# Attention with exponentials on two engines: eleven groups on VectorE instead of ten, and one pass of the last on GpSimd

## The chip, the core and the metric

The kernel runs on one core of a Trainium2 chip. A core has five engines that run side by side, each with its own queue of instructions, in order: TensorE (PE; its weight loads are listed as PEld), VectorE (DVE), ScalarE (ACT), GpSimd (POOL) and SyncE (SP, which issues most DMAs here). They wait for each other through semaphores. The metric is device time in microseconds (us); lower is better. The profile is one execution, recorded by the hardware profiler.

## The reference

Attention over 8 x 8 heads, 512 positions, 64 dimensions, all float32:

```
scale = 1.0 / np.sqrt(q.shape[-1])
scores = np.einsum('bhqd,bhkd->bhqk', q, k) * scale
scores = scores - scores.max(axis=-1, keepdims=True)
attn = np.exp(scores)
attn = attn / attn.sum(axis=-1, keepdims=True)
return np.einsum('bhqk,bhkd->bhqd', attn, v)
```

So there are 64 x 512 x 512 = 16.8 million exponentials. The kernel leaves out the subtraction of the maximum, which cancels in the division.

## The kernel before, in words

**Tiling.** Heads come in 32 pairs. Of a pair, q, k and v are loaded as 128x512 float32 tiles (256 KB each) by SP, and cast to float16 by GpSimd (`cast`, lines 435 and 445). q and k are transposed on TensorE (line 469, eight 128x128 matmuls for a pair) into a PSUM bank and copied to SBUF by VectorE (`copy`, line 482, tile `tqk`). A score block is 128 keys by 512 queries of one head; four blocks make a head. Two blocks make a *group*, 128x1024 scores in a PSUM tile `st` (three buffers). There are 129 groups, numbered from 0; the last two are halves of one (256 queries each), so that the end is short. Groups 0 to 2 are written out by hand (`first_pair`).

**Exponentials.** For most groups ACT computes exp(scale x score) in one instruction from `st` to a float16 tile `pt` (line 516). For the groups in `ON_DVE` (line 34, ten of them) VectorE does it by arithmetic on bits: TensorE first writes a constant into `st` (line 497, the lift) and adds the scores to it; then `raise_` (line 533) scales and clamps `st` into a float32 tile `z`, which frees `st`; then three passes (`pass_`, line 550) form a polynomial of z's low 16 bits: the first (f + c0) x f into `y`, the second (y + c1) x y into `y`, the third c2 x y + z as an integer into `pd`, of which one half of each word is the float16 result. `z` and `y` have two buffers each, `pd` has four.

**Values.** For each head and each quarter of the queries, four matmuls (`values`, line 585) multiply `pt` or `pd` with v, to which a column of ones is appended, so that the sum of the exponentials comes with the output. Seven such units of 65 columns share a PSUM bank; VectorE takes the reciprocal of the sums (line 563) and multiplies (line 565) into a ring in SBUF, and SP stores each finished head from there. The two PSUM banks `x0` and `x1` serve transposes and outputs in turn. The last head has code of its own (`last_values`, line 601, and `finish`, lines 615 and 616).

**What sets the order.** All instructions are emitted in an order that a planner in the kernel's own Python (`Plan`) fixes beforehand: it goes through time in steps of 5 ns with constants for how long each thing takes, and notes when which step would be issued. Its times are not waits: on the chip each engine runs its own instructions in that order, held by data dependences only. PE's steps are chosen in `step_pe` (scores when a buffer is free and ACT's backlog is small, else transposes of a pair up to `AHEAD` ahead, else values). VectorE's are chosen in `step_dve`: first copies that are due, then raises, then the others in order of readiness; passes fill the rest, as long as no other job would be more than `LATE_NORM` or `LATE_COPY` late. GpSimd's casts are placed behind a pass of VectorE, when possible (`emit`, `cast_behind`), and each cast brings with it the load of the pair seven further on, on SP's queue, in which the stores stand too. `EXP` and `EXP_FIXED` are what one exponential on ACT takes in the plan, `SLOT` one group's scores on PE, `PASS` a pass, `port` the time up to which a pass or a cast has SBUF's port in the plan.

Of the kernel before, what the change touches and what calls it, by code (L numbers as in the profile page):

```python
# [16 lines left out]

class Plan:

    SLOT, EXP, EXP_DONE, EXP_FIXED = 216, 853, 181, 50  # L20
    INTO, OUT_OF = 95, 105
    TRANSPOSE, V_UNIT = 225, 130
    TO_ACT, TO_DVE, TO_PE = 220, 210, 60

    COPY, NORM, RAISE = (601, 690), (307, 390), (1132, 1215)
    COPY_1 = (400, 190)
    NORM_COLUMN, PASS_DONE = 67, 80
    PASS, PASSES = 1133, 3
    OFFSET = 216
    FIRST_EXP = 4915  # L30
    STEP = 5
    CALM, KEEN = 14000, 6
    FIRST_UNIT = 4
    ON_DVE = (8, 21, 29, 40, 54, 65, 77, 85, 90, 106)

    LATE_NORM, LATE_COPY, HURRY, SOON, BACKLOG = 600, 1800, 900, 80, 1200
    SLACK, AHEAD = 0, 1

    CAST, CAST_DONE, TO_POOL = 557, 130, 150
    FIRST_LAND, LOAD, STORE, LATENCY, ISSUE = 5200, 700, 350, 2300, 450  # L40
    RAW, QK16, NV = 7, 5, 12

# [68 lines left out]
    def step_pool(self, t):  # L111
        if self.uncast and self.uncast[0][1:] != (1, "q") and not self.casts and self.pool <= t:
            quiet = not self.passes and self.port <= t and not any(x[1] == "raise" for x in self.ready)
            if self.fits(t) and (quiet or self.uncast[0][0] - 1500 < t):
                self.emit(t, None)
        if self.casts and self.pool <= t and self.port <= t:
            g, n, after = self.casts[0]
            if after <= t and self.landed.get((g, n), 1e9) <= t:
                self.casts.pop(0)
                self.pool = t + self.CAST  # L120
                self.port = t + self.CAST
                self.cast_done[(g, n)] = t + self.CAST + self.CAST_DONE
# [153 lines left out]
    def step_dve(self, t):  # L276
        if self.uncast and self.uncast[0][1:] == (1, "q"):
            if self.landed.get((1, "q"), 1e9) <= t:
                self.emit(t, None)
                self.dve = t + 240  # L280
                self.pool = self.port = t + 330
                self.cast_done[(1, "q")] = t + 400
            return
        now = [x for x in self.ready if x[0] <= t]
        if now:
            g = self.groups[min(self.m + 1, len(self.groups) - 1)][0][0]
            job = min(now, key=lambda x: (x[1] != "copy" or x[2][0] > g, x[1] != "raise", x[0]))
            self.ready.remove(job)
            _, kind, what = job
            slots = 2 if kind == "raise" else 1  # L290
            while slots and not self.casts and self.fits(t, 60 if slots == 1 else 0):
                self.emit(t, self.dve_done if self.dve_done > t - 300 else None)
                slots -= 1
                if slots and self.fits(t, 500):
                    self.emit(t, self.dve_done if self.dve_done > t - 300 else None)
                    slots -= 1
            self.note(t, kind, *what)
            if kind == "norm":
                more = self.NORM_COLUMN * what[1]
                self.dve = t + self.NORM[0] + more  # L300
                self.banks[what[2]] = t + self.NORM[1] + more + self.TO_PE
                for _ in range((what[0] + what[1]) // 4 - what[0] // 4):
                    self.loads.append(("store", self.dve + 100))
            elif kind == "finish":
                self.dve = t + self.NORM[0] + 2 * self.NORM_COLUMN
            elif kind == "copy":
                held, done = self.COPY if what[0] != 1 else self.COPY_1
                self.dve = t + held
                self.banks[what[1]] = self.tq[what[0]] = t + done + self.TO_PE
            else:  # L310
                self.dve = t + self.RAISE[0]
                self.read[what[0]] = t + self.RAISE[1] + self.TO_PE
                self.passes += [(what[0], s) for s in range(self.PASSES)]
            self.dve_done = self.dve
        elif self.passes:
            m, s = self.passes[0]
            end = max(t, self.port) + self.PASS
            late = {"copy": self.LATE_COPY, "norm": self.LATE_NORM, "raise": self.LATE_NORM, "finish": 0}
            if all(x[0] > end - late[x[1]] for x in self.ready):
                self.passes.pop(0)  # L320
# [22 lines left out]
def kernel(  # L343
# [7 lines left out]
    nc = tc.nc  # L351
# [191 lines left out]
    def pass_(m, s):  # L543
# [181 lines left out]
    with tc.manual_schedule():  # L725
# [9 lines left out]
        for n in range(NV):  # L735
# [8 lines left out]
            "raise": raise_,  # L744
            "copy": lambda g, b: copy(g),
            "pass": pass_,
            "last": last_values,
            "finish": finish,
            "norm": lambda u, n, b: normalise(u, n),
# [33 lines left out]
```

## Time and profile before

| | us |
|---|---|
| median of three runs | 118.86 (118.70 to 118.92) |
| the profiled execution | 118.68 |
| its span, first to last instruction | 116.9 |
| mean granted clock of TensorE | 1.000 |

Busy times of all engines, the costliest lines and the stages are shown with the prediction. How to read them: a line of the kernel is L and its number; "out<-in" are tiles by the program's names with buffer numbers left out, then partitions x elements and type. "x10" is a count. In a timeline the columns are start and duration in us, then what ran; instructions of one kind that follow each other stand in one row with their count. In a list of waits stand the engine and line, what ended the wait, then us in total, times and the longest. In a table of stages each engine has its busy time and, in brackets, its instructions that start in the stage. In a line's own view stand the shortest, median and longest duration in ns, and below who waited for it (us, times). Records of ACT overlap: an instruction's record begins when its operands are there, while the one ahead still runs.

### The profile page before, as it was taken

The page shows a single profiled execution, that of the slowest core. Times are in us where ns is not written, and L with a number is a line of the kernel's source. Part 1 is how long each engine was busy: PE and PEld are TensorE (multiplying, and loading weights), DVE is VectorE, ACT ScalarE, POOL GpSimd, SP SyncE. Part 2 cuts the span into 40 slices and gives each one's busy share as a digit, 9 for nine tenths or more (in the row PEclk, how much of TensorE's full clock was granted, in tenths as well). Part 3 has the DMA queues.
Part 4 walks back from the last instruction along what each step waited for, and adds up shares of the span by engine and source line. Part 5 has one row for each costly group of instructions (what it writes and reads, how often), then busy time and mean ns, then how long its engine had stood idle before and what let it go on. Part 6 is the DMA issues. An engine that isn't in the chain of part 4 may idle for free.

```text
span 116.9 us, 4082 instructions
## 1 busy us (share of the span) xinstructions
PE 105.0 (90%) x1579; PEld 66.4 (57%) x1579; DVE 98.1 (84%) x174; ACT 110.6 (95%) x123; POOL 57.9 (50%) x102
## 2 busy tenths in 40 slices
PE   7969996987998999898997999999989998999980
PEld 2626553664655666455754575565556665667460
DVE  3453997699899999999999969899978999996281
ACT  4599999999999999999999999999999999999980
POOL 2369925844725844355592595549246454442000
PEclk9999999999999999999999999999999999999999
DMA  3999999999999999999899998899999996232254
GB/s 100 288 374 380 379 383 383 385 376 374 359 338 332 346 346 336 320 303 358 229 327 302 301 299 276 244 325 268 329 356 313 320 309 225 78 117 98 89 176 134
DMA packets 35604, 33.83 MB, mean 289 GB/s; under 512 B 2688, under 2 KB 35584, under 8 KB 35584
## 3 DMA queue, kind: packets, MB, share of 16 engines
q1 hardware_dynamic: 35152, 33.24, 86.9%
q10 hardware_dynamic: 432, 0.33, 0.9%
q8 instruction: 12, 0.20, 0.7%
q14 instruction: 8, 0.07, 0.2%
HBM read 25.17 MB, written 8.39 MB: 287 GB/s over the span
## 4 chain that ended last, share of the span: by engine, by line
ACT 52%; PE 25%; DVE 11%; issue 9%; ACTq 0%
ACT pt L516 50%; PE st L511 9%; PE o L585 9%; DVE y L550 3%; PE st_0a L634 3%; PE tp L469 2%; ACT pt L684 2%; DVE z L533 2%; DVE tqk L482 2%; DVE ring L565 2%; DVE pd L550 1%; PE st L497 1%; DVE rc L563 1%; DVE obl L616 0%; DVE rc_last L615 0%
## 5 line engine op out<-in xcount | busy, mean ns | idle before, releaser
L516 ACT ACTIVATE pt<-st 128x1024 f16<-128x1024 f32 (+1 forms) x116 | 105.7, 1279 | 0.0
L511 PE MATMUL st<-tqk 64*128 64x512 f16 (+1 forms) x250 | 45.6, 380 | 5.2 <-ACT pt L516 3.7
L585 PE MATMUL o<-vp,pt 128*128 128x65 f16 x928 | 42.3, 194 | 0.4 <-DVE tqk L482 0.2
L585 PEld LDWEIGHTS <-pt 128*128 128x128 f16 x928 | 35.6, 98 | 12.0 <-issue 10.9
L445 POOL CAST qkp<-k 128x512 f16<-128x512 f32 x31 | 19.0, 614 | 16.6 <-DVE rc L563 3.9
L435 POOL CAST vp<-v 128x512 f16<-128x512 f32 x32 | 19.6, 616 | 15.4 <-DVE y L550 7.6
L445 POOL CAST qkp<-q 128x512 f16<-128x512 f32 x30 | 18.4, 614 | 13.2 <-DVE pd L550 5.4
L565 DVE TENSOR_TENSOR ring<-o,rc 128x448 f32<-128x448 f32 (+2 forms) x37 | 22.6, 612 | 1.5 <-DVE rc L563 0.3
L511 PEld LDWEIGHTS <-tqk 64*128 64x128 f16 x250 | 13.1, 93 | 18.2 <-issue 10.5
L482 DVE COPY tqk<-tp 128x1024 f16<-128x1024 f16 x30 | 20.5, 683 | 1.0 <-PE tp L469 1.0
L469 PE MATMUL tp<-ident,qkp 128*128 128x128 f16 x248 | 19.9, 220 | 1.2 <-DVE tqk L482 0.6
L469 PEld LDWEIGHTS <-qkp 128*128 128x128 f16 x248 | 14.1, 97 | 9.8 <-issue 4.9
L533 DVE TENSOR_SCALAR z<-st 128x1024 f32<-128x1024 f32 x10 | 12.2, 1221 | 2.5 <-PE st L511 2.2
L563 DVE RECIPROCAL rc<-o 128x7 f32<-128x7 f32 (+2 forms) x37 | 7.4, 199 | 6.8 <-PE o L585 6.4
L550 DVE SCALAR_TENSOR_TENSOR y<-y 128x1024 f32<-128x1024 f32 x10 | 12.4, 1240 | 0.0
L550 DVE SCALAR_TENSOR_TENSOR y<-z 128x1024 f32<-128x1024 uint16 x10 | 12.3, 1232 | 0.1
L550 DVE SCALAR_TENSOR_TENSOR pd<-y,z 128x1024 uint32<-128x1024 f32 x10 | 12.2, 1218 | 0.0
L585 PE MATMUL o<-vp,pd 128*128 128x65 f16 x80 | 11.8, 195 | 0.0
L585 PEld LDWEIGHTS <-pd 128*128 128x128 f16 x80 | 7.8, 98 | 1.5 <-issue 0.8
L497 PE MATMUL st<-const-bfloat16-1.0,lift 64*128 64x512 bf16 x20 | 3.9, 380 | 0.8 <-ACT pt L516 0.6
L634 PE MATMUL st_0a<-const-bfloat16-1.0 128*128 128x512 bf16 (+1 forms) x11 | 3.5, 482 | 0.8 <-PEq L767 0.8
L634 PEld LDWEIGHTS <-const-bfloat16-1.0 128*128 128x128 bf16 x15 | 1.7, 129 | 2.4 <-issue 2.4
(48 smaller groups left out, 22.1 us busy)
## 6 DMA issues: line engine op xcount, KB each, us to landing
out_dram<-ring SPq DMA_DIRECT2D x63, 128.0 KB, 3.9
k<-in_k_dram SPq DMA_DIRECT2D x31, 256.0 KB, 5.3
q<-in_q_dram SPq DMA_DIRECT2D x31, 256.0 KB, 5.1
v<-in_v_dram SPq DMA_DIRECT2D x27, 256.0 KB, 5.4
v<-in_v_dram SPq DMA_DIRECT2D x10, 128.0 KB, 4.0
k<-in_k_dram ACTq DMA_DIRECT2D x2, 128.0 KB, 2.8
q<-in_q_dram SPq DMA_DIRECT2D x2, 128.0 KB, 2.6
out_dram<-obl SPq DMA_DIRECT2D x1, 64.0 KB, 1.6
```

Of the source, the lines that this page charges most:

```text
L435: return nc.gpsimd.tensor_copy(out=vps[g % NV][:, :, :, 0:D], in_=raw[g]["v"][:, :, :, :])
L445: return nc.gpsimd.tensor_copy(out=dst, in_=src[:, :, :, :])
L469: nc.tensor.transpose(tps[g][:, n, i, :], qkp[g][:, n, i, :], ident)
L482: nc.vector.tensor_copy(out=tqk[g][:, :, :], in_=tps.pop(g).rearrange("p n i c -> p n (i c)"))
L511: nc.tensor.matmul(st[:, x, cols], kc, qc[:, cols], start=not on_dve, stop=True)
L516: nc.scalar.activation(out=pt[:, :, cols], in_=st[:, :, cols], func=EXP, scale=scale)
L533: nc.vector.tensor_scalar(out=r["z"][:, :, :], in0=r["st"][:, :, :], scalar1=STEP, scalar2=2.0**17, op0=AluOp.mult, op1=AluOp.max,)
L550: nc.vector.scalar_tensor_tensor(out=r["bits"][:, :, :] if last else r["y"][:, :, :], in0=r["y"][:, :, :] if s else f, scalar=QUARTIC[s], ...
L563: nc.vector.reciprocal(out=rc[:, 0:n], in_=o[:, x : x + n, D : D + 1])
L565: nc.vector.tensor_tensor(out=ring[:, u % NU : u % NU + n, :], in0=o[:, x : x + n, 0:D], in1=rc[:, 0:n].broadcast_to([P, n, D]), op=AluOp. ...
L585: nc.tensor.matmul(os[u // 7][:, u % 7, :], blocks[(g, c, h)][:, y * P : (y + 1) * P], vps[g % NV][:, h, c, :], start=(c == 0), stop=(c == ...
L634: nc.tensor.matmul(dst[:, 0:n], ones[:, 0:P], ones[:, 0:n], start=True, stop=True)
```

## The change

Places and constants in `Plan`; a new job that is planned among GpSimd's casts; and its code. Group 112, the last of the eleven in the new list (`SHARED` = 1), has its middle pass on GpSimd: an addition (`tensor_scalar`, y + c1, times 1.0) into a new tile `t`, and a product of `t` and `y` back into `y`. In the plan that job takes 1000 + 2250 ns, holds the port, and the third pass becomes ready 250 ns behind it. `AHEAD` goes from 1 to 2.

```diff
-    SLOT, EXP, EXP_DONE, EXP_FIXED = 216, 853, 181, 50
-    INTO, OUT_OF = 95, 105
-    TRANSPOSE, V_UNIT = 225, 130
-    TO_ACT, TO_DVE, TO_PE = 220, 210, 60
+    SLOT, EXP, EXP_DONE, EXP_FIXED = 226, 865, 165, 52
+    INTO, OUT_OF = 96, 97
+    TRANSPOSE, V_UNIT = 226, 128
+    TO_ACT, TO_DVE, TO_PE = 206, 215, 60
...
-    PASS, PASSES = 1133, 3
+    PASS, PASSES = 1131, 3
-    FIRST_EXP = 4915
+    FIRST_EXP = 5130
-    ON_DVE = (8, 21, 29, 40, 54, 65, 77, 85, 90, 106)
+    ON_DVE = (7, 20, 28, 40, 51, 56, 70, 80, 84, 98, 112)
+    SHARED = 1
-    LATE_NORM, LATE_COPY, HURRY, SOON, BACKLOG = 600, 1800, 900, 80, 1200
-    SLACK, AHEAD = 0, 1
-    CAST, CAST_DONE, TO_POOL = 557, 130, 150
+    LATE_NORM, LATE_COPY, HURRY, SOON, BACKLOG = 1000, 2200, 900, 80, 1200
+    SLACK, AHEAD = 0, 2
+    CAST, CAST_DONE, TO_POOL = 560, 130, 150
+    MIDDLE, MIDDLE_DONE = (1000, 2250), 250
...
             g, n, after = self.casts[0]
-            if after <= t and self.landed.get((g, n), 1e9) <= t:
+            if g == "middle" and after <= t:
+                self.casts.pop(0)
+                self.pool = self.port = t + sum(self.MIDDLE)
+                self.passes[self.passes.index((n, 2, 1e9))] = (n, 2, self.pool + self.MIDDLE_DONE)
+            elif after <= t and self.landed.get((g, n), 1e9) <= t:
...
-        elif self.passes:
-            m, s = self.passes[0]
+        elif any(x[2] <= t for x in self.passes):
+            m, s, _ = job = next(x for x in self.passes if x[2] <= t)
...
+                if s == 0 and m in self.ON_DVE[len(self.ON_DVE) - self.SHARED :]:
+                    self.passes.remove((m, 1, 0))
+                    self.passes[self.passes.index((m, 2, 0))] = (m, 2, 1e9)
+                    self.casts.append(("middle", m, end + self.TO_POOL))
+                    self.note(end, "middle", m)
...
+    def middle(m):
+        y = raised[m]["y"]
+        t = wpool.tile([P, 2, S], FP32, tag="t", name=f"t_{m}", bufs=1)
+        nc.gpsimd.tensor_scalar(
+            out=t[:, :, :], in0=y[:, :, :], scalar1=QUARTIC[1], scalar2=1.0, op0=AluOp.add, op1=AluOp.mult
+        )
+        nc.gpsimd.tensor_tensor(out=y[:, :, :], in0=t[:, :, :], in1=y[:, :, :], op=AluOp.mult)
```

More of the change, by code (lines that the diff above doesn't have):

```diff
@@ L312, in step_dve @@
                 self.read[what[0]] = t + self.RAISE[1] + self.TO_PE
-                self.passes += [(what[0], s) for s in range(self.PASSES)]
+                self.passes += [(what[0], s, 0) for s in range(self.PASSES)]
             self.dve_done = self.dve
-        elif self.passes:
-            m, s = self.passes[0]
+        elif any(x[2] <= t for x in self.passes):
+            m, s, _ = job = next(x for x in self.passes if x[2] <= t)
             end = max(t, self.port) + self.PASS
@@ L319, in step_dve @@
             if all(x[0] > end - late[x[1]] for x in self.ready):
-                self.passes.pop(0)
+                self.passes.remove(job)
                 self.note(t, "pass", m, s)
                 self.dve = self.port = self.dve_done = end
+                if s == 0 and m in self.ON_DVE[len(self.ON_DVE) - self.SHARED :]:
[3 more added lines that the diff above has]
+                    self.note(end, "middle", m)
                 if s == self.PASSES - 1:
@@ L746 @@
             "pass": pass_,
+            "middle": middle,
             "last": last_values,
```

## The prediction

> **What bounds the kernel now.** I read the page's first part, then the waits and the timeline of ScalarE (ACT), then the instructions of one source line, and last a table of stages. Nothing else than ACT can be the bound if its chain has no holes, so that comes first.
>
> ```profile
> PE 105.0 (90%) x1579; PEld 66.4 (57%) x1579; DVE 98.1 (84%) x174; ACT 110.6 (95%) x123; POOL 57.9 (50%) x102
> ```
>
> ```profile
> ACT L650 <- PEq L767: 1.7, 1, 1.7
> ...
> ACT pt L684 <- PE st_0a L677: 0.4, 1, 0.4
> ```
>
> ```profile
> 6.05 1.95 ACT L684 ACTIVATE pt<-st 128x1024 f16<-128x1024 f32 x2
> 7.86 105.73 ACT L516 ACTIVATE pt<-st 128x1024 f16<-128x1024 f32 x116
> ```
>
> ```profile
> L516 ACT ACTIVATE pt<-st x116: 1017/1293/1501, 7.9 to 112.5; 128x1024 f16<-128x1024 f32 x114, 128x512 f16<-128x512 f32 x2
> ...
>   PE st L511: 3.7, 10
>   PE st L497: 0.6, 2
> ```
>
> ACT's list of waits ends before its first exponentials; for line 516 it has none. The 116 instructions of that line are one stretch of records without a hole, from the end of the two before (6.05+1.95 = 8.00) to 7.86+105.73 = 113.59. Two of them are halves; counted as one, 105.59/115 = 0.918 us is the price of one exponential of 128x1024. A record is longer than that (median 1.293) because it begins while its predecessor still runs: the input was there in time. The reverse wait exists: PE waits for ACT to free a score buffer, 3.7+0.6 us. So the time is: start (8.0), 115 x 0.918, and about 3.3 us of last values, division, store and closing (113.59 to the span's 116.9). The chain view's many pieces of PE and DVE in the middle follow early starts of records; none of them delayed an end.
>
> How near the others are to being the bound, by stage:
>
> ```profile
> core 0: us, PE busy (x) PEld busy (x) DVE busy (x) ACT busy (x) POOL busy (x), PEclk, DMA share, GB/s
> 8.00:24.00 16.00, 14.21 (x208) 8.89 (x208) 11.79 (x19) 15.99 (x18) 11.22 (x20) 1.00 1.09 381
> 24.00:44.00 20.00, 18.27 (x280) 11.86 (x278) 19.15 (x30) 20.00 (x23) 10.78 (x18) 1.00 1.05 353
> 44.00:64.00 20.00, 18.16 (x288) 11.40 (x288) 19.57 (x29) 20.00 (x23) 9.97 (x17) 1.00 0.99 309
> 64.00:84.00 20.00, 18.91 (x290) 11.99 (x290) 18.47 (x30) 20.00 (x24) 12.57 (x22) 1.00 0.94 291
> 84.00:104.00 20.00, 19.09 (x310) 12.53 (x310) 18.61 (x30) 20.00 (x24) 9.57 (x16) 1.00 0.78 255
> 104.00:113.00 9.00, 8.84 (x158) 5.94 (x154) 5.56 (x12) 9.00 (x12) 0.77 (x2) 1.00 0.33 108
> ```
>
> DVE is the neighbour: 75.80 of 80 us from 24 to 104, so 4.20 idle, and 3.44 idle from 104 to 113. What ended its idle time in the long stretch was mostly PE:
>
> ```profile
> DVE rc L563 <- PE o L585: 1.5, 5, 0.6
> DVE tqk L482 <- PE tp L469: 1.0, 1, 1.0
> DVE z L533 <- PE st L511: 0.3, 1, 0.3
> ```
>
> **The change, part by part.** (1) *One exponential of 128x1024 leaves ACT*: -0.92 us, on the path.
>
> (2) *PE* gets one more pair of lift products (line 497) ahead of the group's scores:
>
> ```profile
> 11.30 0.39 PE L497 MATMUL st<-const-bfloat16-1.0,lift 64*128 64x512 bf16 x2
> 11.52 0.70 PE L511 MATMUL st<-tqk 64*128 64x512 f16 x4
> ```
>
> 0.22 us, once. PE's 4.3 us of waiting for ACT hide it, and the 0.92 us by which ACT gets shorter; 3.2 us of that waiting would be left. Without cover it costs its 0.22. Taken as 0.
>
> (3) *DVE* gets a raise (line 533) and two passes (line 550); the third goes to POOL. From the end of the last group's work before:
>
> ```profile
> 86.86 1.22 DVE L550 SCALAR_TENSOR_TENSOR pd<-y,z 128x1024 uint32<-128x1024 f32 x1
> 87.99 0.68 DVE L482 COPY tqk<-tp 128x1024 f16<-128x1024 f16 x1
> ...
> 93.28 1.21 DVE L533 TENSOR_SCALAR z<-st 128x1024 f32<-128x1024 f32 x1
> 94.41 0.68 DVE L482 COPY tqk<-tp 128x1024 f16<-128x1024 f16 x1
> 95.01 1.24 DVE L550 SCALAR_TENSOR_TENSOR y<-y 128x1024 f32<-128x1024 f32 x1
> ...
> 96.94 1.22 DVE L550 SCALAR_TENSOR_TENSOR pd<-y,z 128x1024 uint32<-128x1024 f32 x1
> ...
> 98.68 1.23 DVE L550 SCALAR_TENSOR_TENSOR y<-z 128x1024 f32<-128x1024 uint16 x1
> ...
> 101.66 1.22 DVE L550 SCALAR_TENSOR_TENSOR y<-y 128x1024 f32<-128x1024 f32 x1
> ...
> 104.16 1.21 DVE L550 SCALAR_TENSOR_TENSOR pd<-y,z 128x1024 uint32<-128x1024 f32 x1
> ```
>
> From start to next start a pass or a raise takes 1.13 (86.86 to 87.99, 93.28 to 94.41), so 3 x 1.13 = 3.39 us are added. Old groups 8 and 21 and new groups 7 and 20 lie before 24 us, so the whole added group falls into the long stretch, but for its last pass, which comes behind 104 (below): 2.26 us against an idle 4.20, of which the shorter stretch takes 0.92. Left: 1.02 us of 79, if DVE can use all idle time. Of the idle, 2.8 us was waiting for PE; a backlog of passes fills such holes, and places close together (51 and 56, 80 and 84) make a backlog. Bounds: 0 when every hole is filled, 1.8 us lost when none of the 2.8 can be used (2.8 - 1.02). I take 0.1, near the lower end, because the old kernel already ran 20 us at 19.57 busy without a hole in ACT, with two dense places of its own (77, 85, 90).
>
> (4) *The middle pass on POOL*, addition and product. POOL in this trace has only casts and fills:
>
> ```profile
> 0.24 0.10 POOL L767 MEMSET const-float32-0.0<- 128x1 f32 x1 [0.24 <-issue]
> ...
> 1.01 0.29 POOL masks.py:199 TENSOR_SCALAR_AFFINE_SELECT ident<-ident 128x128 f16<-128x128 f16 x1
> 3.42 0.38 POOL L651 CAST k<-k 128x128 f16<-128x128 f32 x1 [2.12 <-DMA k<-in_k_dram]
> 4.00 0.61 POOL L653 CAST q<-q 128x512 f16<-128x512 f32 x1 [0.20 <-DMA q<-in_q_dram]
> ```
>
> Slope (0.61-0.38)/384 = 0.60 ns an element, so 1024 elements take at least 0.61+512 x 0.60 = 0.92; two such, 1.84, are the lower bound. The upper one lets each of the three streams that are read cost two whole casts: 3 x 1.22 = 3.66. I take 3.2, near the upper, since the product reads two. Where does it lie? New group 112 comes six groups after old group 106; one more of the groups ahead of it is on DVE, so five exponentials, 4.6 us, later: its raise starts near 93.28+4.6 = 97.9. The old group needed 104.16+1.21-93.28 = 12.1 us from raise to last pass, because the passes of the group before it and copies and divisions lay between. Between its first pass's end (98.68+1.23 = 99.91) and its last pass's start (104.16) were 4.25 us, of which the middle pass took 1.13 and other work the rest. POOL's 3.2 fits in these 4.25 beside that work, so the last pass would end at 97.9+12.1-1.13 = 108.9 (109.5 with the upper bound plus hand-overs). Its pair's values follow:
>
> ```profile
> 107.83 0.84 PE L511 MATMUL st<-tqk 64*128 64x512 f16 x4
> ...
> 109.22 1.28 PE L511 MATMUL st<-tqk 64*128 64x512 f16 x4
> 110.43 1.20 PE L585 MATMUL o<-vp,pt 128*128 128x65 f16 x32
> ```
>
> 32 matmuls, 1.20 us, in a tail where ACT ends at 112.7. PE has room there: four of its score matmuls take 1.28 once and 0.84 once, where 0.70 does in the row at 11.52; that is 0.72 us idle. Cost 0, to 1.20 if nothing is hidden; I take 0.05, near 0, since 3.8 us lie between 108.9 and ACT's end.
>
> The Trainium skill (GPSIMD Engine Reference, Performance versus the Vector engine) gives a two-input fp32 addition of 2048 elements 4497 ns on GpSimd against 2293 on VectorE, because two reads share one port. No row here shows a two-input operation on POOL. By half of it the product would take 2.25 and, as an estimate, the sum of the tail would not change. Its section When to use GPSIMD advises against elementwise work of two inputs there for that reason; here VectorE, not GpSimd, is the scarce one by the table of stages.
>
> What is queued behind the middle on POOL are casts:
>
> ```profile
> 102.94 0.61 POOL L445 CAST qkp<-q 128x512 f16<-128x512 f32 x1 [1.48 <-DMA out_dram<-ring]
> 103.54 0.62 POOL L435 CAST vp<-v 128x512 f16<-128x512 f32 x1
> 105.44 0.62 POOL L435 CAST vp<-v 128x512 f16<-128x512 f32 x1 [1.29 <-DVE pd L550]
> ```
>
> POOL was idle 1.48 and 1.29 us before two of them and 9.57 of 20 us busy in that stage; the last query cast could be 3 us late before the scores at 107.83 wait for its transposes. Taken as 0.
>
> (5) *Places, constants, one pair more of transposes ahead, an extra tile* issue nothing of their own; they only reorder. Transposes, copies, casts, and with each cast a load on SP's queue, move up to four groups earlier, past stores in the same queue; stores are not waited for until the ring comes round. DMA engines are less than full after 44 us (309 GB/s and falling against 381). Cost 0 if the loads still land; otherwise a late cast shows as a wait of PE for POOL. It belongs with the bounds of (3).
>
> Sum: -0.92+0.10+0.05 = -0.77. The profiled run took 118.68, so 117.91; the median of the runs is 118.86, 0.18 above it, so 118.09, given as **118.1**.
>
> **Rivals.** *DVE becomes the bound* (slower). Mechanism: PE runs in order and only two PSUM banks are shared by transposes and outputs; a late division or copy holds one, PE stops ahead of the next scores, and ACT gets its first holes. For: 1.02 us of room in 79. Against: copies may now be a pair early, and last raise and pass lie near the end. Price: the 1.8 us of (3), so 118.86-0.92+1.8 = 119.7. It turns slower once the holes cost ACT over 0.92+0.24 us.
>
> *The tail gives the gain back*: the eleventh group ends late, and its 1.20 us of values, or 0.48 beyond PE's idle 0.72, come behind the last exponential; with the middle of the two, 118.86-0.92+0.84 = 118.8. For: 108.9 against 112.7 leaves 3.8 us, and a slow first use of an operation would eat into it; the nearest row is ACT's table load:
>
> ```profile
> 1.66 1.28 ACT L650 ACT_TABLE_LOAD   x1 [1.66 <-PEq L767]
> ```
>
> Against: POOL's own first fill, selection and cast took 0.10, 0.29 and 0.38, none slow.
> The same page of the Trainium skill (GPSIMD Engine Reference, Instruction dispatch) names about 6 us for the first call of a freshly loaded kernel. No row here shows one; by it the last pass would end near 115, behind ACT's end.
>
> *PE becomes the bound*: 0.91 us idle from 84 to 104. It needs 0.22 more and has 0.17 (0.92 x 20/108) less, so 0.5 stays; if that lies in the wrong places, the 0.39 shows on ACT: 118.86-0.92+0.39 = 118.3.
>
> **Chances.** Forecast 0.57; DVE bound 0.24; tail 0.14; PE 0.05. A measurement of this kernel tells about 0.2% (0.24 us) from no change. Faster: forecast and PE, 0.62. Same: 0.13 of the tail's 0.14, whose span of 118.4 to 119.1 straddles that bound. Slower: DVE and the tail's worst, 0.25. Range: low end 117.8 (118.70, the lowest run, less 0.92); high end 119.5, just under the DVE rival's full price. The forecast's own range is 117.8 to 118.5.
>
> **What would show it.** Line 516 with x115 and no ACT wait for PE: (1) right. Records of line 516 near 1.02 in the middle mean ACT started empty: the DVE rival, with PE waiting for DVE's copies or divisions. DVE's idle between 24 and 104 should fall from 4.2 to 1-2 us. POOL's two new instructions should take 1.8 to 3.7 us together, end before 106, and the last pass before 110; values that read pd after ACT's end mean the tail rival. A gap of ACT over 1.2 us in sum would make the forecast wrong.

## The result, and the profile after

| | before | after |
|---|---|---|
| median of 11 runs of each, us | 118.86 | 118.28 |
| ratio after to before, 95% interval | | 0.9959 (0.9940 to 0.9978) |
| the profiled execution, us | 118.68 | 117.88 |
| its span, us | 116.9 | 116.1 |

The change makes the kernel faster by 0.4%, about 0.5 us. One of the 11 runs after was a slow one (123.3 us), which the ratio leaves out. Two later sets of 12 runs, on two chips, gave 0.9954 (0.9935 to 0.9974) and 0.9933 (0.9903 to 0.9963); by these three ratios the gain is 0.49, 0.55 and 0.80 us, 0.6 in the mean. The forecast was 118.1, a gain of 0.77. So the sign and the main term hold, and there is a question left: the profiled pair differs by 0.80, the medians by less.

The changed kernel has its own line numbers. Line 516 (exponential) is now 527, 511 (scores) 522, 497 (lift) 508, 533 (raise) 544, 550 (passes) 561, 482 (copy) 493, 563 and 565 (division) 582 and 584, 445 and 435 (casts) 456 and 446. GpSimd's two new instructions are lines 574 and 577.

First the page's first part, the timeline of ScalarE and the view of line 527, all of the kernel after:

```profile
PE 104.8 (90%) x1581; PEld 66.9 (58%) x1581; DVE 101.4 (87%) x177; ACT 109.7 (95%) x122; POOL 60.5 (52%) x104
```

```profile
7.89 104.86 ACT L527 ACTIVATE pt<-st 128x1024 f16<-128x1024 f32 x115
```

```profile
L527 ACT ACTIVATE pt<-st x115: 717/1232/1418, 7.9 to 112.0; 128x1024 f16<-128x1024 f32 x113, 128x512 f16<-128x512 f32 x2
...
  PE st L522: 3.1, 11
  PE st L508: 0.4, 1
```

115 instead of 116 instructions, again in one stretch. It starts 0.03 us later than before and ends at 7.89+104.86 = 112.75 instead of 113.59, so 0.84 earlier. TensorE's wait for ScalarE shrank from 4.3 to 3.5 us: its queue is still ahead. Behind ScalarE's end the kernel needs 3.32 us (116.06-112.74) where it needed 3.31.

The table of stages after:

```profile
core 0: us, PE busy (x) PEld busy (x) DVE busy (x) ACT busy (x) POOL busy (x), PEclk, DMA share, GB/s
...
24.00:44.00 20.00, 18.98 (x289) 12.14 (x286) 19.80 (x30) 20.00 (x23) 10.31 (x18) 1.00 1.01 331
44.00:64.00 20.00, 18.50 (x281) 11.78 (x282) 19.76 (x28) 19.96 (x23) 9.86 (x17) 1.00 1.00 323
64.00:84.00 20.00, 18.86 (x307) 12.60 (x304) 19.68 (x31) 20.00 (x24) 11.40 (x20) 1.00 0.99 317
84.00:104.00 20.00, 18.61 (x300) 11.85 (x298) 18.93 (x29) 20.00 (x23) 11.51 (x17) 1.00 0.72 237
```

VectorE's idle time from 24 to 104 fell from 4.20 to 1.83 us (80-19.80-19.76-19.68-18.93): the stretch takes the added group in, but not by idle time alone. Between 24 and 104 us begin 28 passes and 9 raises, where it was 26 and 8, and they take 4.2 us more (34.99+10.95 against 32.01+9.76); the divisions take 1.2 us less there, because some of them now run behind 104. One figure is new: ScalarE's 19.96 in the stage from 44 to 64, which is 0.04 us without even a started exponential. More is lost there than the table shows, because records overlap. Line 516 or 527 from 44 to 51, first before, then after:

```profile
L516 ACT ACTIVATE pt<-st x9: 1177/1363/1415, 43.5 to 50.9; 128x1024 f16<-128x1024 f32 x9
```

```profile
L527 ACT ACTIVATE pt<-st x8: 1018/1028/1158, 43.6 to 50.2; 128x1024 f16<-128x1024 f32 x8
```

The columns are the shortest, median and longest record in ns. After, half of them are at about 1.02, the length of an exponential that finds ScalarE free. Before, none is under 1177: each began at least 0.16 us earlier than it had to, so its scores had come in time. There ScalarE lives from hand to mouth.

To measure this, take the *ends* of the exponentials. Where the input is in time, the end of one 128x1024 exponential comes 917 ns after the end of the one before it, to within a few ns, in all traces. What a distance has above 917 is a **hole**: time in which ScalarE had nothing to do. Worked out so from the recorded starts and durations, with exponentials counted from 0:

```
profile            start: end   holes       holes from the         end of the
                   of the 4th   ahead of    12th on (where)        last one
before             7.996        0.116       0                      113.592
before, again      7.949        0           0                      113.430
after              8.030        0           0.153 (45, 49)         112.744
after, again       7.737        0.027       0.262 (45, 49)         112.551
after, third       7.902        0.014       0.556 (20 to 49)       113.023
```

The third column is what lies ahead of the 12th exponential. The kernel before has no hole later than that in either profile; the kernel after has 0.15 to 0.56 us in all three. At exponential 49 it is 0.14 us each time; at 45 it is 0.01, 0.12 and 0.13; the third profile has three more in front of them (0.03 at 20, 0.18 at 38, 0.08 at 42).

Now the eleventh group's passage through GpSimd, the timelines of GpSimd and of VectorE, after:

```profile
101.28 1.04 POOL L574 TENSOR_SCALAR t<-y 128x1024 f32<-128x1024 f32 x1 [1.17 <-DVE y L561]
102.41 2.36 POOL L577 TENSOR_TENSOR y<-t,y 128x1024 f32<-128x1024 f32 x1
104.71 0.61 POOL L446 CAST vp<-v 128x512 f16<-128x512 f32 x1
```

```profile
95.84 1.22 DVE L561 SCALAR_TENSOR_TENSOR pd<-y,z 128x1024 uint32<-128x1024 f32 x1
...
98.34 1.22 DVE L544 TENSOR_SCALAR z<-st 128x1024 f32<-128x1024 f32 x1
99.59 1.60 DVE L561 SCALAR_TENSOR_TENSOR y<-z 128x1024 f32<-128x1024 uint16 x1
...
104.86 1.55 DVE L561 SCALAR_TENSOR_TENSOR pd<-y,z 128x1024 uint32<-128x1024 f32 x1
```

The raise begins at 98.34 (97.9 was forecast) and the last pass ends at 104.86+1.55 = 106.41, 6.3 us ahead of ScalarE's end. The two instructions of GpSimd took 1.04+2.36 = 3.40 us, each at its first and only use. The Trainium skill (GPSIMD Engine Reference, Performance versus the Vector engine) had led to an estimate of 2.25 for the product; the trace has 2.36. Both passes in these rows are much longer than the 1.22 of the others. That leads to the experiments.

### The profile page after: what moved, and what is told of

Same layout as the page of the kernel before. It is cut to its first block, busy times and chain, and to the rows that moved or that the text cites. A ratio compares the mean times of both kernels' runs of the same rounds, so it can differ in the third digit from the quotient of the medians.

```text
span 116.1 us, 4085 instructions
## 1 busy us (share of the span) xinstructions
PE 104.8 (90%) x1581; PEld 66.9 (58%) x1581; DVE 101.4 (87%) x177; ACT 109.7 (95%) x122; POOL 60.5 (52%) x104
## 4 chain that ended last, share of the span: by engine, by line
ACT 31%; DVE 30%; PE 18%; DMA 10%; issue 7%; POOL 1%; SPq 0%; POOLq 0%; ACTq 0%
ACT pt L527 29%; DVE y L561 7%; DVE tqk L493 6%; DMA k<-in_k_dram 6%; DVE z L544 6%; PE st L522 6%; PE o L604 6%; DVE ring L584 5%; DMA v<-in_v_dram 4%; DVE pd L561 4%; PE st_0a L653 3%; ACT pt L703 2%; PE tp L480 2%; POOL qkp L456 1%; DVE rc L582 1%
## 5 line engine op out<-in xcount | busy, mean ns | idle before, releaser
L522 PE MATMUL st<-tqk 64*128 64x512 f16 (+1 forms) x250 | 44.6, 380 | 4.3 <-ACT pt L527 3.1
L604 PE MATMUL o<-vp,pt 128*128 128x65 f16 x920 | 43.0, 194 | 1.4 <-DVE tqk L493 0.9
L604 PEld LDWEIGHTS <-pt 128*128 128x128 f16 x920 | 36.3, 98 | 11.0 <-issue 9.7
L480 PE MATMUL tp<-ident,qkp 128*128 128x128 f16 x248 | 20.5, 220 | 0.6 <-DVE tqk L493 0.2
L561 DVE SCALAR_TENSOR_TENSOR pd<-y,z 128x1024 uint32<-128x1024 f32 x11 | 14.2, 1288 | 0.0
L544 DVE TENSOR_SCALAR z<-st 128x1024 f32<-128x1024 f32 x11 | 13.4, 1217 | 0.9 <-PE st L522 0.9
L561 DVE SCALAR_TENSOR_TENSOR y<-z 128x1024 f32<-128x1024 uint16 x11 | 13.9, 1261 | 0.1
L604 PE MATMUL o<-vp,pd 128*128 128x65 f16 x88 | 13.1, 194 | 0.3 <-DVE pd L561 0.2
L604 PEld LDWEIGHTS <-pd 128*128 128x128 f16 x88 | 8.6, 98 | 3.2 <-issue 2.4
```

The lines of the kernel that those rows point to most:

```text
L480: nc.tensor.transpose(tps[g][:, n, i, :], qkp[g][:, n, i, :], ident)
L522: nc.tensor.matmul(st[:, x, cols], kc, qc[:, cols], start=not on_dve, stop=True)
L544: nc.vector.tensor_scalar(out=r["z"][:, :, :], in0=r["st"][:, :, :], scalar1=STEP, scalar2=2.0**17, op0=AluOp.mult, op1=AluOp.max,)
L561: nc.vector.scalar_tensor_tensor(out=r["bits"][:, :, :] if last else r["y"][:, :, :], in0=r["y"][:, :, :] if s else f, scalar=QUARTIC[s], ...
L604: nc.tensor.matmul(os[u // 7][:, u % 7, :], blocks[(g, c, h)][:, y * P : (y + 1) * P], vps[g % NV][:, h, c, :], start=(c == 0), stop=(c == ...
```

## The experiments

The expectations name their theories by letters. A is the prediction's own account: one exponential less, VectorE just able to take the group, constants free. The others put the missing part, or the gain itself, elsewhere: in lasting holes, in the order that the constants make (C), in a pass and a cast that hinder each other (D).

### Both kernels again, unchanged

> The kernel before, unchanged, for the span and mean granted clock of each of its runs. Profiled so far: before 116.9 us of span at clock 1.000, after 116.1 at 0.992; ScalarE's end moved from 113.59 to 112.74, -0.85, while the medians of all runs differ by 0.58 only. Theory A (the profiled pair tells the whole gain; the rest is when TensorE's clock is raised at the start, which falls differently in each run): the spans of this kernel spread over 0.6 to 0.9 us and follow the mean clock as those of after do (0.993 at 116.1 to 1.000 at 116.9), and at equal clock this kernel is 0.8 to 0.9 above after. Theory B (the busier VectorE makes holes in ScalarE in some runs of after): this kernel's spans spread less than 0.4, and after's upper runs have no counterpart here.

> The changed kernel, unchanged, beside the kernel before on one chip, with a second profile. Theory A: ratio near 0.993 to 0.996; ScalarE's records have under 0.3 us of holes after 12 us in this profile too, and what differs between two profiles of this kernel lies before 12 us. Theory B: holes of 0.3 us or more between 24 and 104 us, behind waits of TensorE for copies or divisions of VectorE.

Before: 118.64 in the median (118.23 to 119.38); after: 118.19 (117.61 to 118.49), ratio 0.9954 (0.9935 to 0.9974). The executions of either kernel spread over about a microsecond, so a pair of profiles is one draw of each. Two of these draws of the kernel after, 117.88 and 117.64, were among its lowest. The holes at exponentials 45 and 49 came back with 0.12 and 0.15, so they belong to the order and not to one execution, though the one at 45 is only 0.01 in the first profile. That the spans follow the mean granted clock was not borne out: at equal clock they scatter as well. The mean of 0.992 in the first profile of the kernel after comes from its end: the granted clock is 1.00 from 8 to 113 us and 0.68 from 113 to 116, where ScalarE is done.

### The middle pass back on VectorE

```diff
-    SHARED = 1
+    SHARED = 0
```

> Eleven groups at the new places, the middle pass of group 112 back on VectorE. Theory A (ScalarE sets the end, the tail has room): within 0.2 us of after, since VectorE has 2.5 us idle from 104 to 113. Theory B (VectorE is at its limit, POOL's help is what makes the eleventh group pay): 0.5 to 1.1 us slower than after, up to the 1.13 of one pass, with the last pass's values behind ScalarE's end.

118.6 (117.93 to 119.85), ratio 0.9985 (0.9963 to 1.0007) against 0.9954 for the change on the same chip: about 0.4 us slower, between what the two theories said (within 0.2, and 0.5 to 1.1). Its late holes are like the change's (0.30 against 0.26 us), and from the end of exponential 3 to the end of the last one it needs the same, 104.85 against 104.81 us, early holes taken off. What differs in the profiles is what comes behind: 3.78 us from ScalarE's end to the span's instead of 3.31. VectorE's timeline of this kernel:

```profile
98.80 1.21 DVE L544 TENSOR_SCALAR z<-st 128x1024 f32<-128x1024 f32 x1
...
102.94 1.22 DVE L561 SCALAR_TENSOR_TENSOR y<-y 128x1024 f32<-128x1024 f32 x1
...
105.45 1.22 DVE L561 SCALAR_TENSOR_TENSOR pd<-y,z 128x1024 uint32<-128x1024 f32 x1
...
112.73 0.18 DVE L582 RECIPROCAL rc<-o 128x4 f32<-128x4 f32 x1 [0.60 <-PE o L604]
```

and of the kernel after:

```profile
111.98 0.18 DVE L582 RECIPROCAL rc<-o 128x4 f32<-128x4 f32 x1 [0.29 <-PE o L604]
```

From the raise to the end of the last pass are 7.87 us here (105.45+1.22-98.80) and 8.07 after, so GpSimd's slower pass costs the group next to nothing. With the middle pass on VectorE the last division ahead of the last head's (four units) starts 0.46 us before ScalarE's end (113.19-112.73) instead of 0.76 (112.74-111.98), but the end is not held by it: the last store is issued 1.02 us behind ScalarE's end here and 0.92 in the kernel after, and lands 2.58 and 2.48 us behind it. So 0.10 of the 0.47 us can be pointed at in the work of the tail. The rest lies behind the last landing, in the closing semaphores (1.20 us here, 0.84 in both profiles that are compared with it), and was not shown to come from the edit. So the pass on GpSimd seems worth about 0.4 us in the runs, and why is open. The start of this execution (below) adds to its time without belonging to the edit.

### Ten groups in the new plan

```diff
-    ON_DVE = (7, 20, 28, 40, 51, 56, 70, 80, 84, 98, 112)
-    SHARED = 1
+    ON_DVE = (7, 22, 27, 43, 56, 73, 79, 83, 97, 102)
+    SHARED = 0
```

> Ten groups only, at places of their own (7, 22, 27, 43, 56, 73, 79, 83, 97, 102), no pass on GpSimd, with the new constants. Theory A: one exponential more on ScalarE, 0.92 us above after, so within 0.3 of the kernel before. Theory C (the constants and the order give the gain): at least half the gain stays, 118.6 or less against 118.86.

120.99 (120.05 to 121.47), ratio 1.0184 (1.0147 to 1.0221), 2.8 us behind the change where one exponential is 0.92. No theory had this. The profile has 1.08 us of holes at exponentials 79 to 96 and 0.39 early. With ten groups at these places the new constants lose. This kernel differs from the one before in places as well as in constants, so it cannot say which of the two loses, and the new constants at the old ten places were not run.

### The constants of before under eleven groups

All of the planner's constants that the diff changes, back at their old values; the eleven places stay:

```diff
-    SLOT, EXP, EXP_DONE, EXP_FIXED = 226, 865, 165, 52
+    SLOT, EXP, EXP_DONE, EXP_FIXED = 216, 853, 181, 50
...
-    LATE_NORM, LATE_COPY, HURRY, SOON, BACKLOG = 1000, 2200, 900, 80, 1200
-    SLACK, AHEAD = 0, 2
+    LATE_NORM, LATE_COPY, HURRY, SOON, BACKLOG = 600, 1800, 900, 80, 1200
+    SLACK, AHEAD = 0, 1
```

> Eleven groups at the new places with the middle pass of the last on GpSimd, but all of the planner's constants of before (also one pair of transposes ahead instead of two). Theory A (constants are free, the places and the exponential make the gain): within 0.3 us of the changed kernel. Theory C (the order that these constants give is what keeps ScalarE fed): holes of ScalarE of over 1 us in sum, slower than before.

122.45 (121.58 to 124.09), ratio 1.0295 (1.0228 to 1.0361). From its list of waits:

```profile
PE st L522 <- DVE tqk L493: 3.4, 5, 1.3
...
ACT pt L527 <- PE st L522: 2.3, 4, 0.8
```

The same instructions, 3.5 us of holes (2.8 of it late). This is the prediction's rival "VectorE becomes the bound" with every link in the open: a copy of transposes is late on VectorE, TensorE stands 1.3 us ahead of its scores, ScalarE runs dry for up to 0.8. The part behind ScalarE's end grows as well, to 4.17 us. And it is slower than the kernel before: the same eleven groups fit in one order and not in the other.

### One pair of transposes ahead instead of two

```diff
-    SLACK, AHEAD = 0, 2
+    SLACK, AHEAD = 0, 1
```

> The changed kernel with transposes only one pair ahead (AHEAD 1). Theory A: within 0.3 us of the changed kernel. Theory C: PE's scores wait for copies of VectorE that come too late, holes of ScalarE of 0.5 us or more, and the gain of 0.5 us is lost.

119.16 (118.93 to 119.93), ratio 1.0046 (1.0020 to 1.0071). Its list of waits:

```profile
PE st L522 <- DVE tqk L493: 1.3, 2, 1.1
...
ACT pt L527 <- PE st L522: 0.4, 2, 0.3
```

1.07 us of late holes; the gain of the exponential is gone and more. It is the same chain as with the old constants, in small; the list of the kernel after has no wait of the scores for a copy of line 493. So the account of the rival C holds for this one number: transposing two pairs ahead is worth about 1 us in this order of eleven groups.

### Where the holes at 45 and 49 come from

Going back from them, the first thing that is late on VectorE is the last pass of group 28. VectorE and GpSimd, kernel after:

```profile
34.94 1.22 DVE L561 SCALAR_TENSOR_TENSOR y<-y 128x1024 f32<-128x1024 f32 x1
36.07 0.68 DVE L493 COPY tqk<-tp 128x1024 f16<-128x1024 f16 x1
...
37.44 1.51 DVE L561 SCALAR_TENSOR_TENSOR pd<-y,z 128x1024 uint32<-128x1024 f32 x1
38.87 1.21 DVE L544 TENSOR_SCALAR z<-st 128x1024 f32<-128x1024 f32 x1
```

```profile
36.70 0.61 POOL L456 CAST qkp<-k 128x512 f16<-128x512 f32 x1 [1.78 <-PE st L522]
37.26 0.61 POOL L456 CAST qkp<-q 128x512 f16<-128x512 f32 x1
```

The casts of pair 12 were planned to lie beside the copy and the division, ahead of that pass. The first starts at 36.70 and the second at 37.26, 0.18 before the pass; the pass takes 1.51 instead of 1.22. In the kernel after, six passes are longer than 1.29 us and together 1.27 us above 1.24 each; in the kernel before, two (1.39 and 1.295), by 0.21. The Trainium skill (SBUF — State Buffer, SBUF: two separate sides) says that a VectorE operation with two inputs in SBUF and a GpSimd operation that reads SBUF use one port pair as an exclusive lock, and that the one which starts first keeps it for its whole instruction while the other is blocked. The traces agree: a pass that starts 0.18, 0.09 or 0.34 us into a cast was recorded with 1.51, 1.60 and 1.35 us. What it is longer by (0.29, 0.38, 0.13) is each time what was left of the cast (0.43, 0.52, 0.27) less 0.14 to 0.15 us; a pass that starts 0.45 us or more into a cast takes at most 1.24.

Four edits aim at this. The first follows the profile's own word, that the cast waited 1.78 us for TensorE's scores, and puts it one place earlier in the order:

```diff
     steps = plan.run()
+    at = steps.index(("cast", 12, "k", True))
+    steps.insert(steps.index(("scores", 38, False)), steps.pop(at))
```

> The changed kernel with one step of the order moved: GpSimd's cast of pair 12's k stands ahead of the scores of group 38 on TensorE instead of behind them. In both profiles of the changed kernel this cast started 0.5 us late, waiting for those scores; the cast of pair 12's q behind it was then still running when VectorE's last pass of group 28 started, which took 1.51 us instead of 1.22; from there VectorE and then TensorE's scores are 0.3 us late, and ScalarE has its only two holes after 12 us, at its exponentials 45 and 49 (0.13 and 0.14, 0.12 and 0.15 us). Theory D (that one collision makes both holes): the pass takes 1.22, both holes are gone or under 0.03 in sum, ratio 0.001 to 0.003 under that of the changed kernel (0.9954). Theory B (VectorE is too full in that stretch whatever the casts do): the holes stay within 0.05 of what they are.

118.4 (lowest 117.78), ratio 0.9960 (0.9930 to 0.9990), no better. GpSimd and VectorE of this kernel, in an execution in which everything runs 0.8 us later since its start:

```profile
37.49 0.62 POOL L456 CAST qkp<-k 128x512 f16<-128x512 f32 x1 [1.78 <-PE st L522]
38.05 0.62 POOL L456 CAST qkp<-q 128x512 f16<-128x512 f32 x1
```

```profile
38.23 1.51 DVE L561 SCALAR_TENSOR_TENSOR pd<-y,z 128x1024 uint32<-128x1024 f32 x1
```

Nothing moved: again 0.18 between cast and pass, again 1.51, again holes of 0.10 and 0.14. So the wait list's "PE st" was not what held the cast, and the edit tested that and not the collision. The kernel's code says why nothing could move: `cast_behind` makes each such cast wait, by a semaphore and beyond its data dependences, for the VectorE instruction that stands last ahead of it in the order. Here that is the middle pass of group 28, which ends at 34.94+1.22 = 36.16 in the kernel after, and the edit does not move the cast past a VectorE instruction.

The second does the same for every k cast, ahead of the TensorE steps that stand directly before it:

```diff
+    for at, step in enumerate(steps):
+        if step[0] == "cast" and step[2] == "k" and step[3]:
+            to = at
+            while steps[to - 1][0] in ("scores", "values", "transposes"):
+                to -= 1
+            steps.insert(to, steps.pop(at))
```

> The changed kernel with every such cast of k (18 of them) moved ahead of the steps of TensorE that stand between it and the VectorE step that it follows. Theory D: of the six passes that took over 1.3 us (1.1 us too much in sum) at most three are left, no hole over 0.05 us after 12 us, time within 0.1 us of the kernel with one cast moved. If casts that start earlier meet other passes, the sum of the passes' excess stays above 0.8 us and new holes appear.

118.16 (117.70 to 118.65), ratio 0.9952 (0.9930 to 0.9974). Six passes stay long, by 1.46 us above 1.24 each, and 0.32 us of holes stay, 0.14 at exponentials 45 and 49 each. A miss for the same reason.

The third moves that one cast further, in front of VectorE's middle pass of group 28, so that it has to wait for that pass and is over before the last one:

```diff
+    at = steps.index(("cast", 12, "k", True))
+    steps.insert(steps.index(("pass", 28, 1)), steps.pop(at))
```

> The changed kernel with the cast of pair 12's k moved further ahead, in front of VectorE's middle pass of group 28, so that it is released (by the division before that pass) just after the pass has started. In the kernel with that cast one place earlier nothing moved: it started 0.54 us behind the pass's end all the same, and the second cast met the last pass, which took 1.51 us. Theory D (a pass and a cast exclude each other, whichever starts first holds the other up; the 0.29 us that VectorE loses at that last pass are what ScalarE lacks at its exponentials 45 and 49): now the cast waits for the middle pass instead, its record ends near the pass's end or it starts there; the middle pass stays at 1.22 to 1.25, the last pass of group 28 takes 1.22, the two holes are gone or under 0.05 us in sum. Theory B (VectorE too full there in any case): holes of 0.1 us or more each stay. If cast and pass merely share a path, the middle pass gets longer by 0.3 or more and the holes stay.

118.0 (117.70 to 118.65), ratio 0.9928 (0.9900 to 0.9956). GpSimd, then VectorE, then line 527 from 44 to 51, of this kernel:

```profile
35.78 1.05 POOL L456 CAST qkp<-k 128x512 f16<-128x512 f32 x1 [0.65 <-DVE ring L584]
37.02 0.61 POOL L456 CAST qkp<-q 128x512 f16<-128x512 f32 x1 [0.19 <-DMA k<-in_k_dram]
```

```profile
35.14 1.22 DVE L561 SCALAR_TENSOR_TENSOR y<-y 128x1024 f32<-128x1024 f32 x1
...
37.65 1.22 DVE L561 SCALAR_TENSOR_TENSOR pd<-y,z 128x1024 uint32<-128x1024 f32 x1
```

```profile
L527 ACT ACTIVATE pt<-st x8: 1018/1092/1138, 43.6 to 50.2; 128x1024 f16<-128x1024 f32 x8
```

Now the cast is the one that starts second: it begins 0.64 us into the middle pass and takes 1.05 instead of 0.61 (0.44 more, with 0.58 of the pass left: again less 0.14), and the pass keeps its 1.22. So does the last pass, with the second cast 0.63 ahead of it, already through. The hole at 45 is gone, that at 49 is 0.045 instead of 0.14.

The fourth leaves the collision and gives VectorE time in front of it: the middle pass of group 28 runs on 384 of its 512 columns.

```diff
+        w = 384 if (m, s) == (28, 1) else S
...
-                out=r["bits"][:, :, :] if last else r["y"][:, :, :],
+                out=(r["bits"] if last else r["y"])[:, :, 0:w],
```

(and the same slice for its inputs)

> The changed kernel with the middle pass of group 28 on 384 of each 512 columns (a quarter of that group's y is left at the first pass's value). That pass then takes about 0.93 us instead of 1.22, which gives VectorE back just the 0.29 us that the collision behind it costs, and leaves the collision itself. Theory D: the last pass of group 28 still takes 1.5 us, but ScalarE's holes at exponentials 45 and 49 are gone or under 0.05 us in sum: VectorE's lateness is what they come from. If they stay at 0.13 and 0.14, they come from something else (a cast or transposes that are late by themselves).

117.95 (117.42 to 118.33), ratio 0.9920 (0.9892 to 0.9949). VectorE of this kernel:

```profile
35.51 0.95 DVE L562 SCALAR_TENSOR_TENSOR y<-y 128x768 f32<-128x768 f32 x1
...
37.76 1.49 DVE L562 SCALAR_TENSOR_TENSOR pd<-y,z 128x1024 uint32<-128x1024 f32 x1
```

The middle pass is 0.27 us shorter, the last pass still collides (1.49), the hole at 45 is gone and that at 49 is 0.075, a little over the 0.05 that was expected. So VectorE's lateness makes these holes, and 0.27 us given back ahead of them halves the one at 49 and closes the other. (Its lines stand one further down, 562 for 561.)

The kernel after on the same chip, as the measure for these two:

> The changed kernel once more, beside the two others on one chip: a third profile and a dozen runs. Theory A with the holes of D: exponentials 45 and 49 have holes of 0.1 to 0.15 us each; from the end of the fourth exponential record to ScalarE's end 104.7 to 104.9 us against 105.5 of the kernel before; ratio 0.994 to 0.997.

118.07 (117.75 to 119.00), ratio 0.9933 (0.9903 to 0.9963). Line 527 from 44 to 51:

```profile
L527 ACT ACTIVATE pt<-st x8: 1017/1024/1042, 43.8 to 50.5; 128x1024 f16<-128x1024 f32 x8
```

Here all eight records are between 1017 and 1042, the barest of the three profiles. Two things came out otherwise than expected: from the end of the fourth exponential to the last one's it needs 105.12 us and not 104.7 to 104.9, because of the holes at 38 and 42, which the other profiles hardly have, and the ratio lies just below the range. At 45 and 49 together it has 0.27 us of holes, the first two profiles 0.15 and 0.26; with the early cast there are 0.045, with the short pass 0.075. The hole at 49 says it best: it lies between 0.139 and 0.145 in all six profiles that keep eleven groups, the new constants and the collision at full length, and 0.045 and 0.075 in the two in which the collision is gone or its cost is given back. So the mechanism of these two holes is shown by two edits of different kinds; what makes those at 38 and 42 was not tried. In time it does not show: 0.9928, 0.9920 and 0.9933 lie within each other's intervals, since a few tenths of a microsecond compete with starts that differ by more.

### The start

The executions part before any of the changed groups has run. GpSimd's first cast of pair 1, in the kernel with all passes on VectorE and in the kernel after, again:

```profile
6.69 0.62 POOL L456 CAST qkp<-k 128x512 f16<-128x512 f32 x1 [2.20 <-DMA k<-in_k_dram]
```

```profile
5.67 0.62 POOL L456 CAST qkp<-k 128x512 f16<-128x512 f32 x1 [1.21 <-DMA k<-in_k_dram]
```

The load of k landed a microsecond later in the first, and ScalarE then had a hole of 0.72 us at exponential 5. The kernel with the cast one place earlier, where that cast started at 7.03, had one of 0.95 there, the first profile of the kernel before (6.46) one of 0.12. No edit touches these loads.

Three other kernels (ten groups, one pair ahead, the short pass) have a hole of 0.39 us at exponential 3 instead. TensorE's first scores of 512 queries, of the ten groups and then of the kernel after:

```profile
5.00 0.64 PE L696 MATMUL st<-qt,kt 64*128 64x512 f16 x2
```

```profile
5.02 0.38 PE L696 MATMUL st<-qt,kt 64*128 64x512 f16 x2
```

They take 0.64 us in those three. Their traces record the full granted clock from 6.3 to 6.7 us on, the ten others from 3.6 to 5.1. So part of the spread is when TensorE's clock is raised, as one expectation above had it; this lies ahead of all that the edits change.

## Why the prediction was right, step by step

**One exponential less, on the path**: right. 115 instructions and, at an equal distance of 917 ns, 0.917 us. ScalarE's end came 0.85 us earlier in the profiled pair: 0.917, less 0.03 of a later start, less 0.04 that the holes grew (0.153 against 0.116). The working read the old records as a stretch without a hole; the ends show 0.116 us at exponential 5, which touching records hide.

**VectorE's room**: the way was right (a late VectorE holds up the scores, and they ScalarE). The count, the size and the source of the loss were not.

The count: the working lets the last pass of the added group fall behind 104 us and takes 2.26 us out of 4.20. But the kernel before has its last pass behind 104 as well (the row at 104.16), so two passes and a raise more begin in the stretch, 3.39 us at the working's price, and 4.20-0.92-3.39 leaves nothing (-0.11) where 1.02 was left. That the group went in with a loss of a few tenths is owed to divisions that the new order runs behind 104, which the working does not have; as far as this sum goes it was luck.

The size: the term was 0.10 us; the three profiles of the changed kernel have 0.15, 0.26 and 0.56 us of late holes, 0.32 in the mean, where the two of the kernel before have none. With 0.32 for 0.10, and the 0.01 that the tail took, the prediction's sum is -0.59; the three gains have a mean of 0.61 and a median of 0.55. Both 0.10 and 0.32 lie inside the bounds of 0 to 1.8.

The source: the bounds were about holes of VectorE that cannot be filled, and the step took a pass at 1.13 us wherever it stands. Six of the changed kernel's passes are held by a cast (two of them, the eleventh group's own, behind the last hole), and the group count alone did not tell this. The row that could have told it stands in the old kernel's view of line 550, where a middle pass reaches 1391 ns with a median of 1221:

```profile
L550 DVE SCALAR_TENSOR_TENSOR y<-y x10: 1214/1221/1391, 16.2 to 101.7; 128x1024 f32<-128x1024 f32 x10
```

The late copies and divisions that the rival named are what the old constants and the single pair ahead brought out in full (2.8 and 1.1 us of late holes).

**TensorE**: 0.22 us more at no cost, right; 3.5 us of waiting for ScalarE are left, 3.2 were expected.

**The middle pass on GpSimd**: 3.40 us against 3.2, between the bounds. Its place was nearly right (the raise 0.4 us later than forecast), the chain behind it was too long: the last pass ends at 106.41 and not at 108.9. The forecast took the 12.1 us of old group 106 from raise to last pass, in which the passes of the group ahead were still running; in the new order that group's last pass is over at 95.84+1.22 = 97.06, before the raise, and the chain takes 8.07.

**The tail**: +0.05 forecast and +0.01 found in the profiled pair, 3.31 and 3.32. Its rival had a condition, the last pass near ScalarE's end, that was never close.

**Constants, places, AHEAD at no cost**: right as they were put together, wrong as a statement on each. They issue nothing, but the same eleven groups take 122.45 in the order by the old constants and 119.16 with one pair ahead. The prediction named this path as a rival (VectorE becomes the bound, 119.7) and gave it 0.24; that the new constants were what kept it away was not argued there, so the zero of this step was luck too. The reverse, the new constants and `AHEAD` with the old ten groups, was not run. The kernel before has no late hole, though, and the same 3.31 us behind ScalarE's end, so an order alone had little there to take away.

**What it said would show**: no wait of line 527 for TensorE is listed, VectorE idles 1.83 us (1 to 2), GpSimd's two end at 104.77 (before 106). The records near 1.02, put down there as the sign of the VectorE rival, did appear, in one place and worth a few tenths instead of 1.8.

**The gap between the profiled pair's 0.80 and the 0.49 of its runs**: with late holes of 0.15 the profiled execution was the one of three with the least. The mean gain of 0.6 agrees with 0.917 less the mean hole of 0.32. That the unprofiled runs have such holes is argued from this and was not seen, and the set with the largest gain (0.80) is the one whose profile had the most (0.56), so one profile doesn't stand for its set.

**Open.** Why the cast of pair 12's k starts at 36.70, 0.54 us behind the pass that releases it. GpSimd's queue has two semaphore instructions ahead of it, and 0.39 us pass between them, 0.39 to 0.41 in all eight profiles with this order, also where the cast is moved ahead of the pass and no signal of TensorE comes in between; ahead of most other such casts of k it is 0.06. The plan has 0.15 us from the release to the cast (`TO_POOL`); with that, as an estimate, the two casts would be over about when the last pass starts (36.16+0.15+0.56+0.61 = 37.48 against 37.44) and would not hold it. What sets the landing of the first loads, and how much of the spread of the runs comes from it. Why the pass on GpSimd is worth its 0.4 us. And whether the early cast is worth the 0.1 to 0.2 us of holes that it closes; no version here beats the changed kernel by more than can be measured.

## What to carry to other kernels

Where records of the bounding engine overlap, its busy share hides holes: measure the distance between *ends* and compare it with the distance in a full stretch. Before counting passes of a second engine as so many times their duration, look at the longest of them, because a partner on the same memory port stretches some, and in an engine that is 98% busy these lengthenings are the first thing to reach the bound. When work is moved onto a nearly full engine, the order is part of the change: try it with the old order as well, since the same instructions cost 4 us more there.

## What the runs showed of the hardware

A pass on VectorE that starts within a cast on GpSimd waits inside its own record: 1.51 us with 0.18 of the cast gone, against 1.22 alone; the other way round the cast has 1.05 instead of 0.61. The later one is longer by what is left of the earlier one less about 0.15 us, so a pass that starts within the last 0.15 us of a cast loses nothing. An addition of 128x1024 float32 with a constant took GpSimd 1.04 us and a product of two such tiles 2.36, without a slow first use. A list of waits can name a wrong releaser: 1.78 us were put down to TensorE's scores, and with the scores moved behind the cast they were still there, to the hundredth. Exponentials of 128x1024 end 917 ns apart in a full stretch, while one that starts behind a hole is recorded with 1023 to 1026 ns and one that finds ScalarE busy with up to 1418.
